# Gated-DeltaNet recurrence of a hybrid decoder block: the chunk inverse applied ahead of the loop, with a new stage order and other buffer counts

## The chip, the core and the metric

The kernel runs on one core of one Trainium2 chip. The metric is the device time of one execution in microseconds (us). Three runs of the kernel before gave a median of 2491.94 us (2491.32 to 2495.54).

## The reference

One decoder layer on 2048 tokens of width 1024. It normalises the input, projects it, and splits the columns between two groups of four heads of 128 columns. One group is a gated DeltaNet, the other a retention with fixed decay. Both outputs go through one output projection; a gated MLP with a causal convolution and a final norm follow. The change lies in the gated DeltaNet, whose core is this (per chunk; `m` is strictly lower triangular):

```python
m = jnp.where(strict, jnp.einsum('nbhik,nbhjk->nbhij', kb, kc) * decay, 0.0)
t_mat = lax.linalg.triangular_solve(eye + m, eye, left_side=True, lower=True, unit_diagonal=True)
u_base = jnp.einsum('nbhij,nbhjv->nbhiv', t_mat, vb)
w_mat = jnp.einsum('nbhij,nbhjk->nbhik', t_mat, kb * jnp.exp(gcum)[..., None])
...
def step(state, inp):
    u = u_b - jnp.einsum('bhck,bhkv->bhcv', w_c, state)
    o = jnp.einsum('bhck,bhkv->bhcv', qd_c, state) + jnp.einsum('bhij,bhjv->bhiv', qk_c, u)
    state = state * cd_c[..., None, None] + jnp.einsum('bhck,bhcv->bhkv', kd_c, u)
    return state, o
```

The state goes from chunk to chunk, so the steps of one head follow each other. Everything outside `step` can be done for all chunks at once.

## The kernel before

The tokens are worked in four blocks of 512, and each block in four chunks of 128 tokens. All products are in float32; the large ones are made of three products of values that are split in a high and a low part (`mm3` and `tokmajor`, three matmuls of 512 columns for each 128x128 tile of weights). After the four blocks come the MLP's up products (`mlp_up`, from about 1190 us on) and its down products (`mlp_down`).

A block consists of named stages, written out by hand in the string `ORDER` (L41): a digit for the block and a name. `pro` loads and norms x; `k0`, `q0`, `kq`, `v0` project for the retention heads and `h0` to `h3` are those heads (`ret_head`); `dec` and `d0` to `d3` make decays; `c0` to `c3` (`gdn_kq`, then `gdn_z`) and `e0` to `e3` (`gdn_v`) project, convolve and transpose keys, queries and values of the DeltaNet heads; `b0`, `b1` (`gdn_base`) and `l0`, `l1` (`gdn_lvls`) invert 1 + m for a pair of heads: 32x32 blocks by POOL, larger ones by small matmuls; `r00` to `r13` (`gdn_rec`) are the steps of the recurrence, first digit the pair, second the chunk; `p0`, `p1` and `G0`, `G1` are the gates and the gated outputs (`gated`), and `W1` to `W7` and `N` the output projection by seven products and the second norm. The string is the order in which the program is written. A scheduler then interleaves the stages on each engine, mostly so that pieces of the large products stand between the steps of the recurrence; each engine works through its own list in order. The numbers in `BUFS` and the constants `NW`, `NST` and `NACC` are caps on how many buffers of a kind are alive at once; tiles get their places from a common pool by lifetime.

A step of the recurrence (`gdn_rec`, L670 to L711) works on the two heads of a pair and has three hops from PE to DVE and back:

- `ks` (L684): keys times state and queries times state, four matmuls of 128x128 by 128. DVE subtracts the first, scaled, from the values `vp` (L687, one instruction for each head). ACT copies the second into the output `o` (L690).
- `wps` (L694): the inverse `TT` times those values, two matmuls. DVE scales the result by `brk` into `u` (L697).
- `sps` (L702): `kd` times `u`, then `A` times `u`, two matmuls each. DVE updates the states `Sst` (L704, one instruction for each head) and adds to `o` (L707). The next step's `ks` needs the states.

In the trace a float32 matmul is two instructions, so that a step shows 8, 4 and 8 of them on PE.

`ret_head` has a chain of its own: `rr` (L783) makes four products, L785 on DVE carries the retention state over the chunks, and each second `ro` matmul (L807) needs one of these states. `gated` multiplies the outputs into the gates (L421, DVE), transposes them (`mxt`, L423, PE), and ACT and DVE combine them into what the output projection `wo` reads through the split `wu` (L875, ACT). `dmat` loads a broadcast of the decays and finishes it on DVE (L492).

Weights come through `load_chunk` (L265). At the first use of a matrix the raw weights are loaded (L280) and split by ACT and DVE (L282, L283); from the use after `keep` becomes true the split parts are also written to DRAM, and later uses load them from there (L276). `NLATE` says how many matrices are not kept at their first use.

Of the kernel before, what the change touches and what calls it, by code (L numbers as in the profile page):

```python
# [10 lines left out]
AF = mybir.ActivationFunctionType  # L11
# [4 lines left out]
NW = 5  # L16
# [6 lines left out]
NST = 4  # L23
NUC = 7
NACC = 7
# [8 lines left out]
NLATE = 3  # L34
NXR = 7
FD = 4
BUFS = {"n1": 8, "ykq": 5, "kv": 4, "NT": 5, "AT": 8, "o": 2, "n2s": 11, "xk": 2, "og": 1, "co": 6, "Cw": 4,
        "wx": 1, "wsq": 3, "wvr": 3, "wvt": 9, "ca": 8, "mix": 10, "D": 8, "rk": 5, "rq": 4, "rv": 8,
        "Ar": 1, "Nb": 6, "rot": 1, "rrow": 7}

ORDER = ("0pro 0k0 0v0 0dec 0d0 0c0 0e0 0q0 0d1 0c1 0e1 0d2 0c2 0e2 0h0 0b0 0h1 0d3 0c3 0e3 0l0 0r00 0b1 "  # L41
# [8 lines left out]
P = 128  # L50
# [155 lines left out]
def mixers(ctx, tc, base, base_used, marks, drp, mm3, gamma, mhalf, n1w, n2w, gcw, gv127, epsr, gnw, n2d, hd,  # L206
# [116 lines left out]
    def small(nm, n=16, bufs=2):  # L323
        if nm not in ring:
            ring[nm] = [pc(bufs, n), 0, bufs]
        e = ring[nm]
        e[1] += 1
        return e[0][:, e[1] % e[2]]
# [13 lines left out]
    def A_items(b, st):  # L342
# [90 lines left out]
        def decays(_):  # L433
# [41 lines left out]
            neg = st["neg"] = small("neg", 16)  # L475
            DVE.tensor_scalar(neg, eg[:, :16], -1.0, None, op0=ALU.mult)
# [31 lines left out]
        def gdn_kq(h):  # L508
            def f(w):
# [19 lines left out]
                if ("brk", h // 2) not in st:  # L529
                    st["brk", h // 2] = small("brk", 8, 5)  # L530
                brk = hd_["brk"] = st["brk", h // 2][:, h % 2 * NT:(h % 2 + 1) * NT]
# [9 lines left out]
                kd = hd_["kd"] = half(hd_, "kv", "kv", 0)  # L541
                for c in range(NT):
                    ACT.activation(kd[:, c * P:(c + 1) * P], ps[:, c * P:(c + 1) * P], AF.Copy,
                                   scale=st["ed"][:, c * NH + h:c * NH + h + 1])
# [4 lines left out]
                for cc in range(2):  # L549
                    ps = mbank("kk")  # L550
                    for c1 in range(2):
                        c = cc * 2 + c1
                        PE.matmul(ps[:, c1 * 256:(c1 + 1) * 256].rearrange("p (a t) -> p a t", a=2),
                                  ykq[:, 0, c * P:(c + 1) * P], ykq[:, :, c * P:(c + 1) * P],
                                  start=True, stop=True)
                    for c1 in range(2):
                        c = cc * 2 + c1
                        DVE.scalar_tensor_tensor(Nt[:, c * P:(c + 1) * P], ps[:, c1 * 256:c1 * 256 + P],
                                                 nbrk[:, c:c + 1], Dm[:, c, :],
                                                 op0=ALU.mult, op1=ALU.mult)  # L560
                        DVE.tensor_tensor(At[:, c * P:(c + 1) * P], ps[:, c1 * 256 + P:c1 * 256 + 256],
                                          Dm[:, c, :], op=ALU.mult)
            return f

        def gdn_v(h):
            def f(w):
# [8 lines left out]
                vp = hd_["vp"] = half(hd_, "kv", "kv", 1)  # L575
# [93 lines left out]

        def gdn_rec(hs, c):  # L670
            def f(_):
# [8 lines left out]
                n = len(hs)  # L680
                ps = rbank("ks")
# [4 lines left out]
                for i, e in enumerate(H):  # L686
                    DVE.scalar_tensor_tensor(e["vp"][:, sl], ps[:, i * P:(i + 1) * P], st["neg"][:, jj[i]:jj[i] + 1],  # L687
                                             e["vp"][:, sl], op0=ALU.mult, op1=ALU.add)
# [3 lines left out]
                ps = rbank("wps")  # L692
                for i, e in enumerate(H):
                    PE.matmul(ps[:, i * P:(i + 1) * P], e["TT"][:, sl], e["vp"][:, sl], start=True, stop=True)  # L694
                h2 = lambda t: t.rearrange("p (i d) -> p i d", i=n)
                u = small("u", n * P, 2)
                DVE.tensor_tensor(h2(u), h2(ps[:, :n * P]),  # L697
                                  h2(st["brk", hs[0] // 2])[:, :, c:c + 1].to_broadcast([P, n, P]), op=ALU.mult)
# [122 lines left out]
        def g2(p):  # L821
            hs = (2 * p, 2 * p + 1)
            rec = [[(None, None, gdn_rec(hs, c))] for c in range(NT)]
            rec[-1].append((None, None, gdn_fin(hs)))
            return {f"l{p}": [(None, None, gdn_lvls(hs))]} | {f"r{p}{c}": r for c, r in enumerate(rec)}
# [456 lines left out]
```

## Time and profile before

| | |
|---|---|
| median of three runs | 2491.94 us |
| the profiled execution, by itself | 2488.28 us |
| its span, first to last instruction | 2486.5 us |
| mean granted TensorE clock | 0.992 |
| DVE busy | 1609.0 us (65%) |
| ACT busy | 997.9 us (40%) |
| POOL busy | 569.5 us (23%) |

The profiled execution took 1.8 us more than its span, and 3.66 us less than the median. In the profile PE is the matmul engine, PEld its weight loads, DVE VectorE, ACT ScalarE, POOL GpSimd. "Idle before" counts the time that an engine stood still ahead of an instruction, and names what ended it. A matmul's shown duration is longer than its turn in a stream, since the next one starts before it has ended.

### The profile page before, as it was taken

Reading aid. Unit: us, or ns where it says so; the run is one execution under the profiler, and the core shown is the slowest. Engines: PE = TensorE matmul, PEld = TensorE weight load, DVE = VectorE, ACT = ScalarE, POOL = GpSimd, SP = SyncE. Lnnn points to the kernel's source line nnn. Section 1 sums busy time; section 2 is a strip of 40 time slices with the busy share of each in tenths; the row PEclk is TensorE's granted clock in tenths of the full one; section 3 lists DMA queues with packets and bytes.
Section 4 is the critical chain, followed back from the end, with each engine's and each line's share of the span. In section 5 each row is a group of like instructions: output and inputs, shape, how many; then the busy total and the mean of one; then the engine's idle time right before and its main releaser. Section 6 shows DMA issues by size and latency. Waiting matters only on the chain. (4 is left out here: it accounts for less than half of the span.)

```text
span 2486.5 us, 35733 instructions
## 1 busy us (share of the span) xinstructions
PE 2413.2 (97%) x12476; PEld 2022.1 (81%) x12476; DVE 1609.0 (65%) x3132; ACT 997.9 (40%) x2149; POOL 569.5 (23%) x891
## 2 busy tenths in 40 slices
PE   8999899999999999998999999999999999999998
PEld 7877787888888978886788888888888888888877
DVE  5864776435653563537899889896556567554794
ACT  6644544434442552335454444442122234333331
POOL 1354146521047105230010000000000002430180
PEclk9999999999999999999999999999999999999999
DMA  8756499764864655645898888777667778764783
GB/s 327 265 195 220 167 338 321 265 220 151 306 214 161 207 211 202 225 146 200 333 342 334 297 300 298 287 280 250 226 241 254 273 268 268 233 207 140 251 275 115
DMA packets 285748, 610.17 MB, mean 245 GB/s; under 512 B 40896, under 2 KB 120960, under 8 KB 285568
## 3 DMA queue, kind: packets, MB, share of 16 engines
q1 hardware_dynamic: 269136, 593.85, 68.0%
q10 hardware_dynamic: 16432, 14.04, 1.8%
q8 instruction: 98, 1.61, 0.3%
q14 instruction: 82, 0.67, 0.1%
HBM read 411.09 MB, written 196.71 MB: 244 GB/s over the span
## 5 line engine op out<-in xcount | busy, mean ns | idle before, releaser
L115 PE MATMUL p<-x,wu 128*128 128x512 f32 x1176 | 458.9, 390 | 3.0 <-DVE x L932 2.9
L114 PE MATMUL p<-x,wu 128*128 128x512 f32 x1176 | 454.1, 391 | 4.2 <-ACT x L931 3.4
L116 PE MATMUL p<-x,wu 128*128 128x512 f32 x1176 | 451.1, 390 | 0.0
L386 PE MATMUL tok<-wc,n 128*128 128x512 f32 (+2 forms) x768 | 276.3, 363 | 11.5 <-ACT n L374 9.3
L387 PE MATMUL tok<-wc,n 128*128 128x512 f32 (+2 forms) x768 | 276.7, 361 | 0.0
L388 PE MATMUL tok<-wc,n 128*128 128x512 f32 (+2 forms) x768 | 274.4, 361 | 0.0
L114 PEld LDWEIGHTS p<-x,wu 128*128 128x128 f32 x1176 | 220.9, 188 | 53.0 <-ACT x L931 6.1
L115 PEld LDWEIGHTS p<-x,wu 128*128 128x128 f32 x1176 | 220.9, 188 | 50.9 <-DVE x L932 5.4
L116 PEld LDWEIGHTS p<-x,wu 128*128 128x128 f32 x1176 | 220.9, 188 | 45.4
L1052 DVE SCALAR_TENSOR_TENSOR acc<-uc,base,acc 128x1022 f32<-128x1022 f32 (+1 forms) x176 | 221.2, 1279 | 39.2 <-ACT acc L1049 37.7
L1010 DVE TENSOR_TENSOR uc<-p,uc 128x512 f32<-128x512 f32 x224 | 153.2, 686 | 134.0 <-PE p L116 131.7
L180 POOL TENSOR_TENSOR vt<-vr 128x512 f32<-128x512 f32 x44 | 69.1, 1573 | 625.2 <-DVE v L201 460.5
L114 PE MATMUL d<-v,uu 128*128 128x512 f32 x448 | 175.1, 391 | 0.0
L115 PE MATMUL d<-v,uu 128*128 128x512 f32 x448 | 175.0, 391 | 0.0
L116 PE MATMUL d<-v,uu 128*128 128x512 f32 x448 | 174.9, 390 | 0.0
L386 PEld LDWEIGHTS tok<-wc,n 128*128 128x128 f32 x768 | 146.3, 191 | 31.9 <-ACT n L374 9.3
L387 PEld LDWEIGHTS tok<-wc,n 128*128 128x128 f32 x768 | 146.6, 191 | 18.8
L388 PEld LDWEIGHTS tok<-wc,n 128*128 128x128 f32 x768 | 145.4, 191 | 19.3
L116 PE MATMUL chm<-n,wc 128*128 128x512 f32 x384 | 151.3, 394 | 0.0
L114 PE MATMUL chm<-n,wc 128*128 128x512 f32 x384 | 151.1, 394 | 0.0
L115 PE MATMUL chm<-n,wc 128*128 128x512 f32 x384 | 151.0, 393 | 0.0
L1057 POOL COPY base<-uc 128x2 f32<-128x2 f32 x44 | 31.9, 725 | 449.2 <-DVE uc L1010 449.2
(248 smaller groups left out, 4841.1 us busy)
## 6 DMA issues: line engine op xcount, KB each, us to landing
wu<-wu SPq DMA_DIRECT2D x308, 512.0 KB, 5.9
wc<-wd SPq DMA_DIRECT2D x168, 512.0 KB, 5.5
wv<-wo SPq DMA_DIRECT2D x84, 512.0 KB, 5.6
wd<-wc SPq DMA_DIRECT2D x60, 512.0 KB, 4.1
ur<-au SPq DMA_DIRECT2D x56, 512.0 KB, 5.8
wur<-in_w_u SPq DMA_DIRECT2D x44, 512.0 KB, 6.1
au<-st SPq DMA_DIRECT2D x88, 256.0 KB, 4.8
vr<-in_w_d SPq DMA_DIRECT2D x44, 512.0 KB, 5.9
```

Source lines behind the costliest of these rows:

```text
L114: PE.matmul(ps, ah, bh, start=(first and i == 0), stop=False, skip_group_check=chk)
L115: PE.matmul(ps, ah, bl, start=False, stop=False, skip_group_check=chk)
L116: PE.matmul(ps, al, bh, start=False, stop=(i == n - 1), skip_group_check=chk)
L180: POOL.tensor_tensor(tt[:, j], a, b_, op=ALU.subtract)
L386: PE.matmul(ps, ah, wh, start=(k == 0), stop=False)
L387: PE.matmul(ps, ah, wl, start=False, stop=False)
L388: PE.matmul(ps, al_, wh, start=False, stop=(k == KT - 1))
L1010: add = lambda o, ps, a: DVE.tensor_tensor(o, ps, a, op=ALU.add)
L1052: DVE.scalar_tensor_tensor(acc[:, t:], u[:, :T2 - t], w, acc[:, t:], op0=ALU.mult, op1=ALU.add)
L1057: POOL.tensor_copy(mhalo[:, ci], u[:, T2 - 2:])
```

## The change

The program's text changes in four places.

**The step has two hops.** A new stage `w0` or `w1` (`gdn_wy`) follows `l0` or `l1`. For each head and all four chunks it multiplies the inverse with decayed keys (`wy`) and with the values (`up`); ACT copies the first over the keys in `ykq`, DVE the second over `vp`. In `gdn_rec` the product `wps` and its scaling are gone, and one subtraction on both heads makes `u`.

**What the keys carry.** `gdn_kq` writes two scaled copies of the transposed keys instead of one: `kg` (by `eg`) for `wy` and `kd` (by `ed` times `brk`). `A` takes the factor `brk`, too. `neg` is no longer made.

**Order.** `ORDER` is another string. Among other moves `w0` and `w1` are put in, `0d2` stands ahead of `0q0`, and `3v0` is moved up ahead of `3k0`.

**Counts.** `NW` 5 to 6, `NST` 4 to 5, `NACC` 7 to 8, `kv` 4 to 5, `o` 2 to 4, `n2s` 11 to 12, `wsq` 3 to 5, `ca` 8 to 10, and `NLATE` 3 to 2: the third matrix (keys and queries of head 0) is kept at its first use.

```diff
-NLATE = 3
+NLATE = 2
...
-            neg = st["neg"] = small("neg", 16)
-            DVE.tensor_scalar(neg, eg[:, :16], -1.0, None, op0=ALU.mult)
...
-                kd = hd_["kd"] = half(hd_, "kv", "kv", 0)
+                eb = small("eb", 4, 5)
+                DVE.tensor_tensor(eb, st["ed"].rearrange("p (t h) -> p h t", h=NH)[:, h], brk, op=ALU.mult)
+                kd = hd_["kd"] = half(st, ("kd", h // 2), "kv", h % 2)
+                kg = hd_["kg"] = half(st, ("kg", h // 2), "kv", h % 2)
                 for c in range(NT):
-                    ACT.activation(kd[:, c * P:(c + 1) * P], ps[:, c * P:(c + 1) * P], AF.Copy,
-                                   scale=st["ed"][:, c * NH + h:c * NH + h + 1])
+                    j = c * NH + h
+                    ACT.activation(kg[:, c * P:(c + 1) * P], ps[:, c * P:(c + 1) * P], AF.Copy, scale=st["eg"][:, j:j + 1])
+                    ACT.activation(kd[:, c * P:(c + 1) * P], ps[:, c * P:(c + 1) * P], AF.Copy, scale=eb[:, c:c + 1])
...
-                        DVE.tensor_tensor(At[:, c * P:(c + 1) * P], ps[:, c1 * 256 + P:c1 * 256 + 256],
-                                          Dm[:, c, :], op=ALU.mult)
+                        DVE.scalar_tensor_tensor(At[:, c * P:(c + 1) * P], ps[:, c1 * 256 + P:c1 * 256 + 256],
+                                                 brk[:, c:c + 1], Dm[:, c, :], op0=ALU.mult, op1=ALU.mult)
...
+        def gdn_wy(hs):
+            def f(_):
+                for h in hs:
+                    e = st["hd", h]
+                    ps, ps1 = mbank("up"), mbank("wy")
+                    for c in range(NT):
+                        sl = slice(c * P, (c + 1) * P)
+                        PE.matmul(ps1[:, sl], e["kg"][:, sl], e["TT"][:, sl], start=True, stop=True)
+                        PE.matmul(ps[:, sl], e["TT"][:, sl], e["vp"][:, sl], start=True, stop=True)
+                    ACT.activation(e["ykq"][:, 0], ps1, AF.Copy)
+                    DVE.tensor_copy(e["vp"], ps)
+            return f
...
-                for i, e in enumerate(H):
-                    DVE.scalar_tensor_tensor(e["vp"][:, sl], ps[:, i * P:(i + 1) * P], st["neg"][:, jj[i]:jj[i] + 1],
-                                             e["vp"][:, sl], op0=ALU.mult, op1=ALU.add)
+                u = small("u", n * P, 2)
+                DVE.tensor_tensor(h2(u), st["vp", hs[0] // 2][:, :, sl], h2(ps[:, :n * P]), op=ALU.subtract)
...
-                ps = rbank("wps")
-                for i, e in enumerate(H):
-                    PE.matmul(ps[:, i * P:(i + 1) * P], e["TT"][:, sl], e["vp"][:, sl], start=True, stop=True)
-                h2 = lambda t: t.rearrange("p (i d) -> p i d", i=n)
-                u = small("u", n * P, 2)
-                DVE.tensor_tensor(h2(u), h2(ps[:, :n * P]),
-                                  h2(st["brk", hs[0] // 2])[:, :, c:c + 1].to_broadcast([P, n, P]), op=ALU.mult)
```

What the new order makes of the lists of the engines is shown at three places.

The first is PE at the end of the recurrence of block 2, second pair (steps `r12` and `r13`). In the kernel before these rows stand there, from the last matmul of a projection (`chm`) to the retention product `rr`:

```order
L116 MATMUL chm<-n_8630,wc 128x512
L694 MATMUL wps<-kv,AT 128x128 x2
L702 MATMUL sps<-pers_1359,kv 128x128 x2
L702 MATMUL sps<-pers_1359,AT 128x128 x2
L684 MATMUL ks<-pers_125,ykq 128x128 x4
L694 MATMUL wps<-kv,AT 128x128 x2
L702 MATMUL sps<-pers_1359,kv 128x128 x2
L702 MATMUL sps<-pers_1359,AT 128x128 x2
L783 MATMUL rr<-rv,rk 128x128 x4
```

In the changed kernel the last `sps` of the same pair stands between matmuls of a projection (`tok`), with `rr` and `rkk` of the retention heads behind it:

```order
L387 MATMUL tok<-wc,n_8693 128x264
L388 MATMUL tok<-wc,n_8693 128x264
L709 MATMUL sps<-pers_1390,kv 128x128 x2
L709 MATMUL sps<-pers_1390,AT 128x128 x2
L386 MATMUL tok<-wc,n_8698 128x264
L790 MATMUL rr<-rv,rk 128x128 x4
L806 MATMUL rkk<-ykq 128x128 x4
L387 MATMUL tok<-wc,n_8698 128x264
```

The groups of the two steps, which followed each other directly, now have projection matmuls between them; the same holds at the end of block 1.

The second is PE at the end of block 3, second pair, where no projection is left (`rtr` and `rkk` belong to a retention head). Before:

```order
L702 MATMUL sps<-pers_1359,AT 128x128 x2
L684 MATMUL ks<-pers_125,ykq 128x128 x4
L799 MATMUL rkk<-ykq 128x128 x4
L694 MATMUL wps<-kv,AT 128x128 x2
L702 MATMUL sps<-pers_1359,kv 128x128 x2
L702 MATMUL sps<-pers_1359,AT 128x128 x2
L684 MATMUL ks<-pers_125,ykq 128x128 x4
L694 MATMUL wps<-kv,AT 128x128 x2
L702 MATMUL sps<-pers_1359,kv 128x128 x2
L702 MATMUL sps<-pers_1359,AT 128x128 x2
L783 MATMUL rr<-rv,rk 128x128 x4
```

Now:

```order
L699 MATMUL ks<-pers_125,ykq 128x128 x4
L806 MATMUL rkk<-ykq 128x128 x4
L709 MATMUL sps<-pers_1390,kv 128x128 x2
L709 MATMUL sps<-pers_1390,AT 128x128 x2
L699 MATMUL ks<-pers_125,ykq 128x128 x4
L709 MATMUL sps<-pers_1390,kv 128x128 x2
L709 MATMUL sps<-pers_1390,AT 128x128 x2
L790 MATMUL rr<-rv,rk 128x128 x4
```

The `wps` rows are gone and the rest stands as before, without other work between.

The third is DVE at the end of block 0. L785 (L792 after the change) carries a retention state, L492 (L490) works on the decays of block 1 that a DMA brings, L421 multiplies outputs into gates. Before:

```order
L785 SCALAR_TENSOR_TENSOR pers_605<-pers_125,rr 128x128
L492 SCALAR_TENSOR_TENSOR D<-D,pers_230,base 128x128 x8
L719 SCALAR_TENSOR_TENSOR pers_605<-pers_605 128x8
L492 SCALAR_TENSOR_TENSOR D<-D,pers_230,base 128x128 x2
L785 SCALAR_TENSOR_TENSOR pers_605<-pers_605,rr 128x128
L492 SCALAR_TENSOR_TENSOR D<-D,pers_230,base 128x128 x6
L785 SCALAR_TENSOR_TENSOR pers_605<-pers_605,rr 128x128
L421 SCALAR_TENSOR_TENSOR mix<-o,pers_605,mix 128x128 x8
L785 SCALAR_TENSOR_TENSOR pers_125<-pers_605,rr 128x128
```

Now:

```order
L792 SCALAR_TENSOR_TENSOR pers_612<-pers_125,rr 128x128
L468 COPY pers_230<-pers_230 128x16
L470 TENSOR_TENSOR pers_230<-pers_230 128x16
L792 SCALAR_TENSOR_TENSOR pers_612<-pers_612,rr 128x128 x2
L421 SCALAR_TENSOR_TENSOR mix<-o,pers_612,mix 128x128 x4
L792 SCALAR_TENSOR_TENSOR pers_125<-pers_612,rr 128x128
L478 COPY pers_230<-gct 16x128
L421 SCALAR_TENSOR_TENSOR mix<-o,pers_612,mix 128x128 x8
```

The four links of the retention state now stand ahead of all work on the decays (L490), whose first row comes seven rows further down.

More of the change, by code (lines that the diff above doesn't have):

```diff
@@ L14 @@
 DRAM = bass.MemoryType.DRAM
-NW = 5
+NW = 6
 LA = 1
@@ L22 @@
 NWUR = 2
-NST = 4
+NST = 5
 NUC = 7
-NACC = 7
+NACC = 8
 NWU = 9
@@ L33 @@
 NRAW = 3
-NLATE = 3
+NLATE = 2
 NXR = 7
 FD = 4
-BUFS = {"n1": 8, "ykq": 5, "kv": 4, "NT": 5, "AT": 8, "o": 2, "n2s": 11, "xk": 2, "og": 1, "co": 6, "Cw": 4,
-        "wx": 1, "wsq": 3, "wvr": 3, "wvt": 9, "ca": 8, "mix": 10, "D": 8, "rk": 5, "rq": 4, "rv": 8,
+BUFS = {"n1": 8, "ykq": 5, "kv": 5, "NT": 5, "AT": 8, "o": 4, "n2s": 12, "xk": 2, "og": 1, "co": 6, "Cw": 4,
+        "wx": 1, "wsq": 5, "wvr": 3, "wvt": 9, "ca": 10, "mix": 10, "D": 8, "rk": 5, "rq": 4, "rv": 8,
         "Ar": 1, "Nb": 6, "rot": 1, "rrow": 7}
-ORDER = ("0pro 0k0 0v0 0dec 0d0 0c0 0e0 0q0 0d1 0c1 0e1 0d2 0c2 0e2 0h0 0b0 0h1 0d3 0c3 0e3 0l0 0r00 0b1 "
[8 rows of a table removed]
+ORDER = ("0pro 0k0 0v0 0dec 0d0 0c0 0e0 0d2 0q0 0d1 0c1 0e1 0c2 0e2 0d3 0h0 0b0 0h1 0c3 0l0 0w0 0b1 0r00 "
[8 rows of a table added]
 P = 128
@@ L528, in f @@
                 DVE.tensor_scalar(ss, ss, EPS, None, op0=ALU.add)
-                if ("brk", h // 2) not in st:
-                    st["brk", h // 2] = small("brk", 8, 5)
-                brk = hd_["brk"] = st["brk", h // 2][:, h % 2 * NT:(h % 2 + 1) * NT]
+                brk = hd_["brk"] = small("brk", 4, 8)
                 nbrk = hd_["nbrk"] = small("nbrk", 4, 8)
@@ L574, in f @@
                     PE.transpose(ps[:, c * P:(c + 1) * P], acc[:, c * P:(c + 1) * P], ident)
-                vp = hd_["vp"] = half(hd_, "kv", "kv", 1)
+                vp = hd_["vp"] = half(st, ("vp", h // 2), "kv", h % 2)
                 for c in range(NT):
@@ L680, in f @@
                 n = len(hs)
+                h2 = lambda t: t.rearrange("p (i d) -> p i d", i=n)
                 ps = rbank("ks")
@@ L824, in g2 @@
             rec[-1].append((None, None, gdn_fin(hs)))
-            return {f"l{p}": [(None, None, gdn_lvls(hs))]} | {f"r{p}{c}": r for c, r in enumerate(rec)}
+            return {f"l{p}": [(None, None, gdn_lvls(hs))], f"w{p}": [(None, None, gdn_wy(hs))]} | {f"r{p}{c}": r for c, r in enumerate(rec)}
         def rh(h):
```

16 rows, old and new, of the table ORDER are left out of this document.

## The prediction

> **What bounds the kernel now.** I read the page's first lines, then the busy time by stretches, then PE's idle time by group, then single places in order of time.
>
> ```profile
> span 2486.5 us, 35733 instructions
> PE 2413.2 (97%) x12476; PEld 2022.1 (81%) x12476; DVE 1609.0 (65%) x3132; ACT 997.9 (40%) x2149; POOL 569.5 (23%) x891
> ```
>
> PE is the bound: it is busy for 97% of the span and stands still for 73.3 us. The stretches (columns: PE, weight loads, DVE, ACT, POOL, then granted clock, DMA share, GB/s) say where.
>
> ```profile
> 0.00:1190.00 1190.00, 1130.83 (x6830) 963.13 (x6831) 673.79 (x1861) 532.65 (x1459) 401.93 (x750) 0.99 0.65 230
> 1190.00:2430.00 1240.00, 1233.46 (x5432) 1018.79 (x5431) 912.01 (x1233) 456.14 (x668) 163.18 (x133) 1.00 0.77 267
> 50.00:100.00 50.00, 50.00 (x280) 43.61 (x278) 39.13 (x94) 31.80 (x81) 6.41 (x10) 1.00 0.84 286
> 200.00:250.00 50.00, 45.45 (x349) 39.12 (x349) 27.14 (x70) 24.06 (x66) 18.25 (x46) 0.93 0.52 180
> 250.00:300.00 50.00, 38.60 (x256) 34.53 (x255) 33.34 (x127) 29.34 (x86) 8.47 (x12) 0.90 0.43 158
> 850.00:900.00 50.00, 44.30 (x269) 38.00 (x268) 33.31 (x110) 27.69 (x77) 5.95 (x8) 0.97 0.40 137
> 1100.00:1150.00 50.00, 44.08 (x399) 38.91 (x398) 25.18 (x80) 24.22 (x81) 2.66 (x2) 1.00 0.18 64
> 1150.00:1200.00 50.00, 40.55 (x171) 29.82 (x171) 44.83 (x90) 28.28 (x62) 2.64 (x2) 0.97 0.89 335
> ```
>
> Up to 1190 us, where the mixers end, PE idles 59.2 us; behind that 6.5 us in 1240. The idle time sits at the ends of the blocks (200 to 300, 850 to 900, 1100 to 1200), where the projections have run out and the recurrence is left with nothing to fill its hops. There the clock falls below 1 too. So the MLP stays as it is, and the mixers decide. Next, PE's idle time by group and by what ended it (us in total, times, longest):
>
> ```profile
> L684 PE MATMUL ks<-pers,ykq 128*128 128x128 f32 x256 | 35.8, 282 | 7.4 <-DVE pers L704 3.7 <-DVE AT L561 1.3 <-DVE o L707 1.1
> L694 PE MATMUL wps<-kv,AT 128*128 128x128 f32 x128 | 21.9, 293 | 4.5 <-DVE kv L687 3.1 <-ACT o L690 1.4
> L702 PE MATMUL sps<-pers,kv 128*128 128x128 f32 x128 | 20.6, 283 | 6.3 <-DVE pers L697 5.3 <-ACT o L690 0.6 <-DVE pers L476 0.4
> ...
> PE tok L386 <- ACT n L374: 9.3, 1, 9.3
> PE wo L114 <- ACT wu L875: 6.3, 4, 1.9
> PE ro L807 <- DVE pers L785: 5.8, 5, 2.9
> PE mxt L423 <- DVE mix L421: 3.6, 4, 1.6
> PE ro L806 <- DVE Ar L800: 1.5, 1, 1.5
> ```
>
> The recurrence has 7.4 + 4.5 + 6.3 = 18.2 us; 9.3 us is the start of the program.
>
> **The change part by part.** First, what is added on PE. Per pair of heads and chunk `wps` had two matmuls and `wy` with `up` have four; with 4 blocks, 2 pairs and 4 chunks that is 64 more, or 128 instructions, as the trace shows two for each. Their price comes from one unfilled step in block 3:
>
> ```profile
> 1116.67 1.16 PE L684 MATMUL ks<-pers,ykq 128*128 128x128 f32 x8
> 1117.87 0.61 DVE L687 SCALAR_TENSOR_TENSOR kv<-ks,pers,kv 128x128 f32<-128x128 f32 x2 [0.34 <-PE ks L684]
> 1118.36 0.68 PE L694 MATMUL wps<-kv,AT 128*128 128x128 f32 x4 [0.54 <-DVE kv L687]
> 1119.08 0.42 DVE L697 TENSOR_TENSOR pers<-wps,pers 128x256 f32<-128x256 f32 x1 [0.61 <-PE wps L694]
> 1119.56 0.71 PE L702 MATMUL sps<-pers,kv 128*128 128x128 f32 x4 [0.52 <-DVE pers L697]
> 1121.16 1.20 PE L684 MATMUL ks<-pers,ykq 128*128 128x128 f32 x8 [0.44 <-DVE pers L704]
> 1125.09 1.06 PE L783 MATMUL rr<-rv,rk 128*128 128x128 f32 x8
> ```
>
> The eight of `rr` run in 1.06 us; one alone lasts 0.28 (the `ks` row), so the next starts (1.06 - 0.28) / 7 = 0.112 us later. 128 x 0.112 = **14.3 us more PE work**. Nothing hides it, since PE is the bound.
>
> The same rows give what a hop costs without filler. From `ks` to `ks` pass 1121.16 - 1116.67 = 4.49 us, in which 8 + 4 + 8 = 20 instructions take 2.24. So 2.25 us are lost while the brackets show 0.54 + 0.52 + 0.44 = 1.50: a stop costs 1.5 times its idle time, since the last matmul drains. The recurrence's 18.2 us stand for 27 us lost, about 36 unfilled hops of 0.75.
>
> How many are left? At the ends of blocks 1 and 2 the new list of PE has projection work between all groups; its steps need fillers for two hops, not three, and the projections last longer. At the end of block 3 the list still has bare hops (`ks` to `sps`, `sps` to `ks`, `ks` to `sps`), at the end of block 0 three or four, and `wy` stands close behind the last level of the inverse twice. I count 10 or 11, 8 us. **Gain 19 us**; from 6.8 (only the 4.5 of `wps` go, times 1.5) to 27.
>
> Second, other waits at these ends, which the new lists fill or reorder:
>
> ```profile
> 282.23 0.49 PE L807 MATMUL ro<-pers,ykq 128*128 128x128 f32 x2 [1.46 <-DVE pers L785]
> 285.82 0.79 PE L807 MATMUL ro<-pers,ykq 128*128 128x128 f32 x2 [2.89 <-DVE pers L785]
> 283.83 1.14 DVE L492 SCALAR_TENSOR_TENSOR D<-D,pers,base 128x128 f32<-128x128 f32 x4 [0.61 <-DMA D<-gdr]
> 888.51 1.06 PE L423 MATMUL mxt<-base,mix 128*128 128x128 f32 x8 [0.70 <-DVE mix L421]
> 891.51 0.50 PE L114 MATMUL wo<-wv,wu 128*128 128x512 f32 x1 [1.94 <-ACT wu L875]
> ```
>
> In block 0 `ro` waits since L785 is queued behind decays that wait for a DMA; in the new DVE list it stands ahead of them: 4.4 us back. In block 2 `chm` matmuls now stand between `mxt` and `wo`: 2.6 us back. With the 1.5 of L800, which now has `tok` matmuls to cover it, I take **9 us**; from 0 to 12.
>
> Third, the clock. The rows 0.93, 0.90, 0.97 and 0.97 above lack (0.07 + 0.10 + 0.03 + 0.03) x 50 = 11.5 us of PE cycles, part of them while PE stood still anyway. If half of the stops go I take back **6 us**; from 0 to 11.5. The Trainium skill, "TensorE: Matmul & The Clock Gate" (What's actually happening), gives an idle window of about 3.4 us as what halves the clock. The trace disagrees in so far as no wait of PE but the first is longer than 2.89 us, and the clock fell in four stretches; by the page's threshold those stops would not be the cause and this term would be 0.
>
> Fourth, the costs beside PE. ACT gets 64 copies for `kg` and 16 of 128x512 for `wy`; DVE loses 64 + 32 instructions and gets 32 + 16.
>
> ```profile
> L690 ACT ACTIVATE o<-ks,pers 128x128 f32<-128x128 f32 x64 | 20.1, 367 | 42.5 <-DVE kv L687 38.6 <-issue 2.5 <-DVE pers L719 0.7
> L809 ACT ACTIVATE o<-ro 128x512 f32<-128x512 f32 x16 | 9.5, 592 | 10.9 <-PE ro L807 10.9
> L687 DVE SCALAR_TENSOR_TENSOR kv<-ks,pers,kv 128x128 f32<-128x128 f32 x64 | 19.5, 345 | 30.7 <-PE ks L684 30.5
> L697 DVE TENSOR_TENSOR pers<-wps,pers 128x256 f32<-128x256 f32 x32 | 13.5, 422 | 34.7 <-PE wps L694 34.6
> L505 DVE TENSOR_TENSOR ca<-chm,rrow 128x512 f32<-128x512 f32 x48 | 33.0, 688 | 34.9 <-PE chm L116 32.1 <-ACT pers L526 1.6 <-ACT ykq L519 0.8
> L558 DVE SCALAR_TENSOR_TENSOR NT<-kk,pers,D 128x128 f32<-128x128 f32 x64 | 22.0, 343 | 1.1
> L561 DVE TENSOR_TENSOR AT<-kk,D 128x128 f32<-128x128 f32 x64 | 17.9, 280 | 0.0
> ```
>
> ACT: 64 x 0.367 + 16 x 0.592 = +33 us, beside 533 of 1190 busy. DVE: -64 x 0.345 - 32 x 0.422, then +32 x 0.422, 16 x 0.688 and 64 x (0.343 - 0.280) for `A`: -7 us. Both lie under PE's projections. But `kd` now needs `brk`, thus the squares of keys and queries, and holds the bank with the transposed keys that long; behind it wait the next transposes and ACT's queue. The new lists differ in thousands of rows and will have stops of their own. By the rows from nothing to as many as `wo`, `mxt` and L800 have now (6.3 + 3.6 + 1.5, with drain 17); I take **7 us**, near the `wo` row.
>
> Fifth, `NLATE`: 4 x 512 KB are written in block 0 instead of block 1, where the DMA engines were busy for 0.84 and moved 286 GB/s (50 to 100 us); 2.1 MB take 7.3 us of them. The sixth buffer of `NW` covers part; in block 1 two raw loads, four splits on ACT and DVE go, which PE did not wait for. **2 us**, from 0 to 7. The other counts I cost at nothing, since PE waits on no DMA in these rows and a free buffer can only start a load earlier; if the lists needed them, that is in the waits above.
>
> The sum: 14.3 - 19 - 9 - 6 + 7 + 2 = -10.7 us on the execution's 2488.3 us (span 2486.5 and 1.8 around it): 2477.6. That execution lies 3.7 us under the median of 2491.9, so I forecast **2481 us**.
>
> **The rivals.** *The removed hop was hidden, and the work is not.* Where fillers stand, a hop costs nothing, and 2 of 3 hops remain where they don't. If only the waits ahead of `wps` go (6.8 us) and the rest stays as it is, the time is 2488.3 + 14.3 - 6.8 = 2495.8, or 2499 beside the median: slower. It decides from the point where less than 14.3 us of stops are won. For it: the row of `wps` has only 4.5 us. Against it: the lists, where the groups at the ends of blocks 1 and 2 no longer touch.
>
> *The stops move.* ACT's 33 us and the longer hold on the transposes cost 1 us for each of 16 heads-in-blocks: 7 becomes 16, and 2490 follows, no change. Against it: ACT has over half its time free.
>
> *The clock stays.* The stops that remain still trip it, and the 6 us are not won: 2487, at the border of no change. For it: blocks 0 and 3 keep bare hops. Against it: a block end without stops, such as the new one of block 2, leaves nothing to trip it. By the threshold of the Trainium skill's page above, the short stops that go were not what tripped it, and the time would be this one.
>
> *All of it comes.* The fillers close all hops but 4 us' worth, the clock is back: 14.3 - 23 - 12 - 9 + 4 = -25.7, so 2466. For it: the stops are few and in places where the list has changed.
>
> **How the numbers follow.** A measurement of this kernel tells about 0.2% (5 us) from no change. Chances: forecast 0.48, all of it 0.14, the clock stays 0.14 (half faster, half the same), the stops move 0.09, the hidden hop 0.15. Faster 0.48 + 0.14 + 0.07 = 0.69, same 0.16, slower 0.15. The range leaves out half of the outermost cases on both sides: 2467 to 2498.
>
> **What would show it.** PE's busy work: 128 more instructions in `wy` and `up`, the sum of instructions 12604. The idle rows of `ks` and `sps` should fall from 13.7 to about 6 us and no `wps` row be left; 850 to 900 should be busy at clock 1.00; L807's wait should shrink to under 2 us; PE's idle up to the MLP to about 35 us. I am wrong if that idle time stays near 59 us, if a row of `kqtr`, `chm` or `tok` waiting on ACT appears with several us, or if the first 100 us lengthen.

## The result and the profile after

The changed kernel takes 2496.74 us (median of 20 runs, 2490.44 to 2504.17) against 2491.03 us for the kernel before (20 runs on the same chip): a ratio of **1.0025, with a 95% interval of 1.0016 to 1.0034**, slower by 0.25%. The forecast was 2481 us, faster. The time lies inside the range, but on the other side of no change.

The head of the page of the changed kernel:

```profile
span 2493.8 us, 36020 instructions
PE 2427.1 (97%) x12604; PEld 2035.8 (82%) x12604; DVE 1606.6 (64%) x3092; ACT 1026.8 (41%) x2227; POOL 586.9 (24%) x891
```

PE is busy for 13.9 us more than before (2427.1 against 2413.2), and the span is 7.3 us longer: 6.6 us of idle time were won, where the sum had counted on 25 us of stops and clock. The busy time by stretches of the changed kernel, for the stretches that the prediction quoted and those that changed most (columns: length, then PE, weight loads, DVE, ACT, POOL, then granted clock, DMA share, GB/s):

```profile
0.00:1190.00 1190.00, 1140.29 (x6955) 976.71 (x6956) 668.66 (x1816) 559.93 (x1535) 409.79 (x750) 0.99 0.65 229
1190.00:2430.00 1240.00, 1230.68 (x5418) 1013.47 (x5416) 909.26 (x1230) 454.14 (x665) 172.11 (x132) 1.00 0.77 267
250.00:300.00 50.00, 44.61 (x322) 39.84 (x322) 40.46 (x143) 34.39 (x101) 9.29 (x13) 1.00 0.42 156
350.00:400.00 50.00, 47.71 (x213) 38.94 (x212) 36.97 (x81) 25.51 (x75) 13.97 (x14) 0.97 0.84 301
600.00:650.00 50.00, 47.75 (x229) 39.97 (x228) 31.89 (x90) 24.97 (x63) 2.65 (x2) 0.93 0.67 235
850.00:900.00 50.00, 50.00 (x354) 46.30 (x353) 16.80 (x61) 22.67 (x77) 5.00 (x5) 1.00 0.43 143
1000.00:1050.00 50.00, 47.83 (x237) 39.47 (x236) 21.73 (x68) 24.05 (x81) 18.35 (x40) 1.00 0.63 223
1100.00:1150.00 50.00, 48.60 (x418) 43.76 (x417) 21.34 (x61) 25.20 (x78) 2.77 (x3) 1.00 0.29 102
```

Three of these stretches of the kernel before, which the prediction had not looked at because nothing was lost in them or they seemed untouched:

```profile
350.00:400.00 50.00, 50.00 (x232) 41.48 (x232) 42.10 (x86) 26.78 (x75) 15.48 (x15) 1.00 0.92 329
600.00:650.00 50.00, 48.04 (x244) 40.05 (x245) 36.36 (x108) 26.48 (x71) 4.14 (x4) 1.00 0.76 265
1000.00:1050.00 50.00, 50.00 (x251) 42.30 (x250) 21.79 (x77) 19.11 (x62) 11.69 (x20) 1.00 0.67 228
```

The block ends that the prediction aimed at are better: 38.60 of 50 us busy became 44.61 (250 to 300), 44.30 became 50.00 (850 to 900), 44.08 became 48.60 (1100 to 1150). But 350 to 400 and 1000 to 1050 had no gap before and have one now, and the clock falls at 600. The idle time up to 1190 us went from 59.2 to 49.7 us, not to the 35 us that the prediction named; in the MLP behind it, it rose from 6.5 to 9.3.

To compare stretches in which both work and clock differ, I use one measure below. Each shape of matmul instruction has an undisturbed distance to the start of the next one, read from filled stretches (0.2265 us with 512 columns, 0.1195 with 264, 0.111 with 128, less for the small ones). **PE work** is the sum of these distances over all PE instructions of a trace, and **lost time** is what the starts lie further apart than that: waits, the drain around them, and half clock together. Before: 2361.3 us of work and 108.2 lost. After: 2375.5 and 100.8. So the work grew by 14.2 us and the loss shrank by 7.4; with 0.6 us of later start that is the 7.3 us of span. Lost us by stretch, where it moved by 1 us or more:

| stretch from | 10 | 100 | 150 | 200 | 250 | 350 | 400 | 450 | 500 | 550 | 600 | 850 | 1000 | 1100 | 1150 | 1200 | 1250 |
|---|---|---|---|---|---|---|---|---|---|---|---|---|---|---|---|---|---|
| before | 2.4 | 2.0 | 4.0 | 9.2 | 18.3 | 0.2 | 5.7 | 2.5 | 1.3 | 4.0 | 3.3 | 9.9 | 0.2 | 10.7 | 15.5 | 1.4 | 2.1 |
| after | 1.4 | 0.3 | 7.6 | 8.1 | 8.9 | 4.6 | 8.0 | 4.7 | 2.7 | 1.3 | 5.9 | 0.4 | 3.4 | 3.3 | 17.3 | 3.4 | 3.3 |

(The last stretch runs to 2400 us.) All falls together are 34 us, all rises 26. The prediction had 19 + 9 + 6 = 34 us of falls and 7 + 2 = 9 of rises.

The recurrence itself, in the groups of PE of the changed kernel (busy us, mean ns | idle us ahead, and what ended it):

```profile
L699 PE MATMUL ks<-pers,ykq 128*128 128x128 f32 x256 | 35.7, 276 | 1.2 <-DVE pers L711 1.1
L709 PE MATMUL sps<-pers,kv 128*128 128x128 f32 x128 | 20.7, 285 | 2.7 <-ACT o L704 1.4 <-DVE pers L702 1.3
```

18.2 us of idle time in three groups became 3.9 in two. What PE waits for now (total us, times, longest):

```profile
PE mxt L423 <- DVE mix L421: 5.5, 3, 2.7
PE p L115 <- DVE x L939: 4.5, 5, 1.9
PE wo L115 <- DVE wv L201: 4.4, 1, 4.4
PE ro L813 <- DVE Ar L807: 3.7, 2, 3.1
PE wo L114 <- ACT wu L882: 3.5, 2, 2.2
PE chm L114 <- DVE ca L503: 2.1, 1, 2.1
PE vtr L574 <- DVE AT L561: 1.5, 1, 1.5
```

None of these is the recurrence. Several are single waits of 1.5 to 4.4 us, and but for `vtr`, which waits for `A`, they are in operations that the change does not touch. The longest of them, at 447 us, shows how such a wait is read. First PE, then DVE ahead of it, in the changed kernel:

```profile
446.77 0.80 PE L115 MATMUL wo<-wv,wu 128*128 128x512 f32 x1 [4.42 <-DVE wv L201]
```

```profile
441.26 0.21 DVE L338 SCALAR_TENSOR_TENSOR ca<-pers,base,ca 128x1 f32<-128x1 f32 x1
443.53 0.71 DVE L621 STREAM_TRANSPOSE NT<-AT 128x512 f32<-128x512 f32 x1 [2.06 <-DMA AT<-z]
444.16 0.81 DVE L334 SCALAR_TENSOR_TENSOR ca<-ca,base 128x510 f32<-128x510 f32 x1
444.90 1.21 DVE L338 SCALAR_TENSOR_TENSOR ca<-pers,base,ca 128x2 f32<-128x2 f32 x1
446.04 0.68 DVE L201 TENSOR_TENSOR wv<-wvt,wv 128x512 fp32r<-128x512 f32 x1
```

PE needs L201, the low half of a split weight. It stands on DVE behind a transpose that waits 2.06 us for the DMA of the inverse's base, and behind two steps of a convolution. DVE is busy for 64% of the span, and still PE waits for it: an engine that takes its instructions in order holds whatever stands behind a wait. How much of the 4.42 us that hold is worth, e14 tells below.

### The profile page after: what moved, and what is told of

Same layout as the page of the kernel before. It is cut to its first block, busy times and chain, and to the rows that moved or that the text cites. A ratio compares the mean times of both kernels' runs of the same rounds, so it can differ in the third digit from the quotient of the medians.

```text
span 2493.8 us, 36020 instructions
## 1 busy us (share of the span) xinstructions
PE 2427.1 (97%) x12604; PEld 2035.8 (82%) x12604; DVE 1606.6 (64%) x3092; ACT 1026.8 (41%) x2227; POOL 586.9 (24%) x891
## 5 line engine op out<-in xcount | busy, mean ns | idle before, releaser
L115 PE MATMUL p<-x,wu 128*128 128x512 f32 x1176 | 458.6, 390 | 4.5 <-DVE x L939 4.5
L115 PEld LDWEIGHTS p<-x,wu 128*128 128x128 f32 x1176 | 220.9, 188 | 52.7 <-DVE x L939 7.3
L115 PE MATMUL d<-v,uu 128*128 128x512 f32 x448 | 175.2, 391 | 0.0
L115 PE MATMUL chm<-n,wc 128*128 128x512 f32 x384 | 151.9, 396 | 0.0
L1064 POOL COPY base<-uc 128x2 f32<-128x2 f32 x44 | 41.6, 946 | 444.6 <-DVE uc L1017 444.6
```

What stands on the lines that cost most here:

```text
L115: PE.matmul(ps, ah, bl, start=False, stop=False, skip_group_check=chk)
L1064: POOL.tensor_copy(mhalo[:, ci], u[:, T2 - 2:])
```

## The experiments

All ratios are to the kernel before, run beside it, with the 95% interval; PE work and lost time (us) are those of one profiled execution each. Thirteen kernels ran.

In most of them the scheduler laid the engines' lists anew, because an instruction or a step of `ORDER` had changed. Of the 12348 PE instructions that e9 shares with the kernel before, some 2600 stand in another place in its trace; in e6 it is some 1900 of 12476, in e7, against the changed kernel, some 3600 of 12348. So these runs don't change one thing alone. e11 and e14 come close to that (50 to 75 of 12604 against the changed kernel).

| kernel | hops | ratio | PE work | lost |
|---|---|---|---|---|
| before | 3 | 1 | 2361.3 | 108.2 |
| after | 2 | 1.0025 | 2375.5 | 100.8 |
| e1: new code, old order and counts | 2 | 1.0149 | 2375.5 | 128.2 |
| e3: new code and counts, old order | 2 | 1.0321 | 2375.5 | 176.0 |
| e4: new code and order, old counts | 2 | 1.0044 | 2375.5 | 110.3 |
| e2: old code, new order and counts | 3 | 1.0048 | 2361.3 | 122.7 |
| e5: after with `NLATE` 3 | 2 | 1.0072 | 2375.5 | 117.8 |
| e6: before with unread products | 3 | 1.0164 | 2389.7 | 123.9 |
| e7: after without `wy` and `up` | 2 | 0.9900 | 2347.1 | 98.8 |
| e9: before without `wps` | 2 | 0.9906 | 2347.1 | 103.5 |
| e10 to e13: after, one thing moved | 2 | 1.0019 to 1.0092 | 2375.5 | 98.2 to 114.0 |
| e14: after, one DMA not awaited | 2 | 1.0011 | 2375.5 | 98.2 |

**The two parts alone: e9, e7, e6.** The first takes the third hop out of the program and adds nothing to it:

```
-                    DVE.scalar_tensor_tensor(e["vp"][:, sl], ps[:, i * P:(i + 1) * P], ...)
+                    DVE.scalar_tensor_tensor(u[:, i * P:(i + 1) * P], ps[:, i * P:(i + 1) * P], ...)
...
-                ps = rbank("wps")
-                for i, e in enumerate(H):
-                    PE.matmul(ps[:, i * P:(i + 1) * P], e["TT"][:, sl], e["vp"][:, sl], start=True, stop=True)
-                DVE.tensor_tensor(h2(u), h2(ps[:, :n * P]), ..., op=ALU.mult)
```

> The kernel before, old order and counts, with the inverse's product and the scaling by brk left out of the step, so that it has two hops and 128 PE instructions less: part of the computation is left out. The work alone is 14.3 us. If removing the hop wins the stops that the prediction counts (18 to 20 us, and the clock), 33 to 40 us less than before (2452 to 2458); if the hop was hidden, 14 to 20 us less (2472 to 2477).

Measured: 2467.83 us, ratio 0.9906 (0.9893 to 0.9919), 22.6 us under the kernel before beside it. Of these 14.2 us are the 128 PE instructions that are gone, so **the hop as a stop, together with the lists that come of leaving it out, was worth some 8 us**: 6 to 12 by the interval, 5 by lost time in the one profiled execution. That lies between the two expectations. Its waits are nearly gone, but others came or grew: `wo` at 281 us (2.7), `p` at 1146 us (3.7) and, in the middle of block 1, `tok` at 478 us (3.5). PE's waits in e9, then the one recurrence group of note:

```profile
PE wo L114 <- ACT wu L870: 8.6, 6, 2.7
PE p L114 <- ACT x L926: 5.9, 3, 3.7
PE tok L386 <- DVE rq L734: 3.5, 1, 3.5
PE rkk L794 <- ACT ykq L789: 3.3, 2, 2.2
```

```profile
L684 PE MATMUL ks<-pers,ykq 128*128 128x128 f32 x256 | 35.3, 281 | 3.1 <-DVE pers L699 1.8 <-DVE AT L561 1.2
```

The row of `ks` fell from 7.4 to 3.1 us, `sps` from 6.3 to 0.4, and the 4.5 of `wps` are gone: 15 us of idle time. Lost time ahead of these groups fell by 19 us, from 29.6 to 10.2. The total lost only fell from 108.2 to 103.5. The stretches from 200 to 310 us and from 840 to 940 lost 14 us less; those from 400 to 500 and from 560 to 640 and the MLP lost some 10 more.

e7 takes the products out of the changed kernel, so that `ykq` and `vp` are read unmultiplied:

```
-            return {f"l{p}": [...], f"w{p}": [(None, None, gdn_wy(hs))]} | ...
+            return {f"l{p}": [...], f"w{p}": []} | ...
```

> The changed kernel without the products ahead of the recurrence and their copies, so that keys and values enter the steps without the inverse: part of the computation is left out. 256 instructions less on PE: 28.7 us less than the changed kernel (2468) if all of their work is on the path; 2475 or more if they fill stops or if the lists differ by themselves.

Measured: 2464.00 us, ratio 0.9900 (0.9886 to 0.9914). That is 0.0125 or 31 us under the changed kernel, for 28.4 us of work, so the products cost their work in full. The lost time stays in sum (98.8 against 100.8), but not in its places: the waits at 367 and 447 us are gone, and others at 410, 414, 470 and 1007 us have come. A two-hop kernel without the products loses as much in stops.

e6 adds the same number of products, whose result nothing reads, to the kernel before:

```
+            PE.matmul(ps1[:, sl], e["kd"][:, sl], e["TT"][:, sl], start=True, stop=True)
+            PE.matmul(ps[:, sl], e["TT"][:, sl], e["vp"][:, sl], start=True, stop=True)
```

> The kernel before, with 128 matmuls of 128x128 by 128 for each of the two products added behind l0 and l1, whose results are not read: 256 instructions of each kind, 512 of PE in all where the change adds a net 128. By the step of 0.112 us the whole is 28.7 us for 256 instructions; both theories expect 26 to 30 us more than before if nothing hides it, and 20 or less if the products fill bare hops.

The expectation counts the instructions twice over: the page shows 12732 on PE, 256 more than before. Measured: 2531.16 us, 1.0164 (1.0151 to 1.0178), or 41 us, more than either theory. The profiled execution is 44 us over that of the kernel before, of which 28.4 are work and 16 more lost time. The work is hidden nowhere, and an order that was not made for it adds stops.

As a sum, -22.6 (e9) + 28.4 (the products' work) is +5.8 us, and the change measures +5.7. That they agree is luck as far as these runs tell: e1 below, the same two parts in the old order, measures +37 us, and e6 alone +41.

**Code, order and counts: e1, e3, e4, e2.** e1 has the new functions with the old `ORDER` and counts (the new steps `w0`, `w1` directly behind `l0`, `l1`), e3 the new counts with that order, e4 the new order with the old counts; e2 leaves the functions and takes the new order (without `w`) and counts.

```
e1: ORDER = <before, "l0 w0", "l1 w1">; NW, NST, NACC, NLATE, BUFS of before but "kv": 5
e3: ORDER = <before, "l0 w0", "l1 w1">
e4: NW, NST, NACC, NLATE, BUFS of before but "kv": 5
e2: the kernel before with ORDER of after without w0, w1; NW, NST, NACC, NLATE, BUFS of after
```

> Two hops with the old order (w0 and w1 put in right behind l0 and l1) and the old counts (kv 5, which the pairwise tiles need). Theory A, the new lists brought the stops that ate the gain: 14.3 us of work, some 18 us of recurrence stops won, no other change, so 0 to 8 us faster than before (ratio 0.997 to 1.000). Theory B, the removed hop was hidden and the work is not: 6 to 14 us slower (1.0025 to 1.006).

> Two hops with the old order (w0, w1 behind l0, l1) and the new counts. Theory A1, the order is what the two-hop step needs: as slow as two hops with old order and old counts, 30 us or more over before (1.012 or more). Theory A2, the counts are what it needs: within 10 us of before (0.998 to 1.004).

> Two hops with the new order and the old counts (kv 5). Theory A1, the order decides: within 6 us of the changed kernel (1.000 to 1.005 of before). Theory A2, the counts decide: 20 us or more over before (1.008 or more).

> Three hops as before, with the new order (without w0 and w1) and the new counts. Theory A: slower than before by the stops that the new lists bring, 8 to 15 us (1.003 to 1.006). Theory B: within 4 us of before (0.9985 to 1.0015), since order and counts do little.

Measured: e1 2527.40 us (1.0135 to 1.0163), e3 2570.43 us (1.0308 to 1.0335), e4 2502.58 us (1.0033 to 1.0056), e2 2502.65 us (1.0034 to 1.0061). e1 is slower than both of its theories; the others are where their first theory put them. The order, not the code, sets whether the stops are won: with the old order the two-hop step loses 20 to 68 us more than three hops did. Behind the start of the program, these rows hold the longest wait of e1 and that of e3:

```profile
PE sps L701 <- ACT o L696: 10.0, 3, 7.6
```

```profile
PE nps L909 <- ACT n2s L910: 40.9, 3, 36.5
```

In both PE waits for ACT, and ACT for something else; the rows of ACT, e1 and then e3:

```profile
218.77 0.62 ACT L696 ACTIVATE o<-ks,pers 128x128 f32<-128x128 f32 x2 [14.31 <-POOL pers L600]
```

```profile
540.32 1.26 ACT L910 ACTIVATE n2s<-nps,base 128x512 f32<-128x512 f32 x2 [34.69 <-POOL pers L600]
```

L600 is a line of POOL's loop of 31 steps for the base of an inverse: the trace names it for both, while neither of the ACT rows reads its result. Its last row in e1 is the last that reads `Nb`, the copy of the matrix that is inverted:

```profile
218.53 0.21 POOL L600 TENSOR_TENSOR pers<-Nb,pers 128x8 f32<-128x8 f32 x1
```

It ends at 218.74 us, and ACT starts at 218.77; in e3 the last one ends at 540.29 and ACT starts at 540.32. `o`, `n2s` and `Nb` are tiles of one size from one pool. So the rows fit a wait for the place that `Nb` had held, and not for the inverse. The trace doesn't say which place a tile got, so this stays a reading.

With the new order the counts are worth 0.0019 (e4 against after). The new order doesn't help the old code either: e2 loses 14.5 us more than before. With the order of the other code, three hops cost 12 us more and two hops 31 (e1, which has the old counts, too) or 74 (e3). That each order is fitted to its code is my reading of these four runs; how the orders were found is not on record.

**`NLATE`: e5.** The changed kernel with `NLATE = 3`.

> The changed kernel with NLATE back at 3, so that the third matrix is not written in block 0. If the early writes cost what the prediction took, 2 us less than the changed kernel (2495); if the writes are behind the stops between 150 and 250 us, 5 to 8 us less (2489); if only the lists are laid anew, anything within 10 us.

Measured: 2509.23 us, 1.0072 (1.006 to 1.0083), 12 us over the changed kernel and outside all three expectations. Lost time rose by 17 us, nearly all of it between 100 and 550 us, a time in which many lists were laid anew. The term of the prediction (2 us that `NLATE` 2 costs) had the wrong sign in this order; as a price of the DMA traffic it could not be told from the lists that it lays anew.

**One instruction moved: e10.** The split behind which PE waits at 447 us goes to POOL:

```
-    v = split_v(nc, mk("v", F32R), src)
+    v = split_v(nc, mk("v", F32R), src, kept is not None and i == 4 and k == 1)
...
-    nc.vector.tensor_tensor(v[:, 1], src, ...)
+    (nc.gpsimd if pool else nc.vector).tensor_tensor(v[:, 1], src, ...)
```

> The changed kernel with one instruction moved: the low half of one wv split (block 0, product 4, k 1) is made by POOL instead of by DVE. In the changed kernel PE waits 4.42 us for it at 447 us (wo L115 behind DVE L201), because it stands on DVE behind a transpose that waits for the DMA of the inverse's base. Theory (the new stops come from in-order queues in which something that waits for a DMA stands ahead of what PE needs): that wait shrinks to under 1 us, lost time from 400 to 500 us falls from 12.7 to about 8 us, and up to 2430 PE instructions the rest of the stretches up to 1190 us stays as it is within 3 us; in total 0 to 5 us less than the changed kernel. Rival (DVE's queue is not the cause, PE would wait for something else at the same place): the wait is there under another name, and 400 to 500 us loses 12 us or more as before.

Measured: 2506.54 us, 1.0072 (1.0058 to 1.0086). PE in e10:

```profile
446.12 0.50 PE L115 MATMUL wo<-wv,wu 128*128 128x512 f32 x1 [1.60 <-POOL wv L201]
451.12 1.11 PE L521 MATMUL kqtr<-base,ykq 128*128 128x128 f32 x4 [3.82 <-ACT ykq L517]
```

The wait shrank from 4.42 to 1.60 us (expected: under 1), and 5 us later PE waits 3.82 us for the convolution that stands behind the same transposes. 400 to 500 us loses 14.9 us instead of 12.7: the rival was right on the stretch. The other 10 us of the total came behind 1250 us (13.7 lost instead of 3.3), in the MLP, whose entry was laid anew in the lists though nothing in it was meant to change.

**The hold taken away: e14.** The two transposes of block 1, pair 0 read a matrix that is there already, which leaves the right inverse of that pair out:

```
-                    DVE.transpose(T, TT)
+                    DVE.transpose(T, hd_["N"] if (b, p) == (1, 0) else TT)
```

> The changed kernel in which the two transposes of the inverse's base (L621) of block 1, pair 0 read the matrix N, ready long before, and not the base that comes by DMA: this leaves the right inverse of that pair out, with as many instructions as before. In the lists these two transposes stand 75 and 150 rows of DVE earlier and the rest around 450 us is as it was. Theory (one hold: DVE waits 2.06 us for that DMA ahead of the convolution and the split that PE needs): the 4.42 us wait of wo L115 at 447 us shrinks to 2 us or less, no wait of kqtr takes its place, 400 to 500 us loses 9 us or less instead of 12.7, and the kernel is 3 to 5 us faster than the changed one. Rival (the stretch is short of ready work in any case, or the split waits for ACT and POOL): wo L115 or a neighbour waits 4 us or more as before, 400 to 500 us loses 12 us or more.

Measured: 2492.64 us, 1.0011 (1.0002 to 1.002). PE in e14, and its stretches:

```profile
447.27 0.50 PE L115 MATMUL wo<-wv,wu 128*128 128x512 f32 x1 [2.73 <-DVE wv L201]
...
449.76 1.11 PE L521 MATMUL kqtr<-base,ykq 128*128 128x128 f32 x4 [1.29 <-ACT ykq L517]
```

```profile
400.00:450.00 50.00, 44.29 (x220) 36.73 (x219) 26.51 (x56) 20.74 (x58) 43.85 (x74) 0.99 0.69 230
450.00:500.00 50.00, 50.00 (x324) 41.13 (x324) 21.27 (x73) 15.22 (x41) 21.98 (x38) 0.95 0.73 274
```

Between the theories: lost time in 400 to 500 us is 10.9 (expected 9 or less, rival 12 or more). The hold makes up 1.7 of the 4.42 us; the other 2.73 remain, for the split still stands behind the convolution, which began when `chm` was done. The wait at 457 us (`vtr`, 1.5) is gone. So the DMA hold is one cause, worth 1.7 us of this wait; that the stretch has too little ready work around it is the likely other, which no run tested by itself. The whole kernel is no faster than e11 below, which keeps the hold (1.0019, the intervals overlap).

**Other orders nearby: e11, e12, e13.** One step of the changed kernel's `ORDER` moved, the rest left:

```
e11: "1d2 1b0 1e3 0W4 1c2 1e2 1h0"  ->  "1d2 1e3 0W4 1c2 1e2 1h0 1b0"
e12: "1dec 0G1"  ->  "0G1 1dec"
e13: "0w0 0b1 0r00 0e3"  ->  "0w0 0r00 0e3 0b1"
```

> The changed kernel with one step of ORDER moved: 1b0 stands behind 1h0 instead of ahead of 1e3. The instruction lists differ from the changed kernel's in some twenty rows of DVE, ACT and POOL around 450 us and at the entry of the MLP. Theory (the time hangs on the places of single instructions): within 6 us of the changed kernel, with the difference in the stretches 400 to 500 and 1150 to 1250 us; one direction or the other. Rival (only the code's dependences count): within 2 us, and no stretch differs by more than 1 us.

> The changed kernel with two neighbours of ORDER swapped: 0G1 ahead of 1dec. All lists are laid anew from about 290 us to 500 us and at the entry of the MLP, with the same work. Theory (any new laying of these lists has stops of its own, some 20 us over a list that was searched for): the stops at 365 and 447 us go or change, others come, lost time stays between 95 and 115 us, time 2490 to 2508. Rival (the changed kernel's order is as good as before's, and the new stops belong to the two-hop code): the same stops at the same places, time within 3 us of the changed kernel.

> The changed kernel with one step of ORDER moved: 0b1 stands behind 0e3, not behind 0w0. All lists are laid anew from about 160 us on, with the same work. Theory (any new laying has stops of its own): the stops at 163, 284, 365 and 447 us go or change and others come; lost time 95 to 120 us, time 2490 to 2513. Rival (the stops belong to the two-hop code): the same stops by name, time within 3 us of the changed kernel.

Measured: 1.0019 (1.001 to 1.0028), 1.0043 (1.0031 to 1.0056) and 1.0092 (1.0078 to 1.0106), with 98.2, 106.0 and 114.0 us lost. e11, in which some 75 PE rows stand elsewhere, is the changed kernel again. In e12 the stop at 365 us went (350 to 400: 0.2 us lost instead of 4.6) and 5.1 us came between 300 and 350; in e13 350 to 450 loses 2.2 instead of 12.6, and 500 to 550 12.2 instead of 2.7, where this wait of e13 has come:

```profile
PE nps L917 <- ACT n2s L918: 8.1, 3, 4.2
```

Not all stops move: `ro` still waits for `Ar` at 166 us in e12. The same work loses 98 to 114 us in these three orders and the changed kernel's, mostly in places that move, so most of the new stops belong to how the lists fall and not to the two-hop code as such. No order tried makes the two-hop code faster than the kernel before; whether one exists stays open.

## Why the prediction was wrong, point by point

*PE work, 14.3 us more:* right (14.2 by the distances, 13.9 in busy time), and hidden nowhere (e6, e7).

*The recurrence, 19 us back:* right. Idle time of its groups fell from 18.2 to 3.9 us, which at 1.5 is 21 us; lost time ahead of them fell by 22, from 29.6 to 7.6. No `wps` row is left, and `ks` with `sps` went from 13.7 to 3.9 where about 6 was expected.

*Other waits at the block ends, 9 us:* half right. The wait of `ro` for the retention state is gone, so are those of `mxt` and `wo` at 888 to 892 us, and 850 to 900 is full at clock 1.00. But `ro` for `Ar`, which was to be covered, grew from 1.5 to 3.7 us, and `mxt` now waits 1.2 and 2.7 us at the end of block 0. These rows with `wo` for `wu` went from 17.2 us of idle time to 12.7, so 4.5 came back. That all falls by stretch come to 34 us, as the first three terms did, is partly luck: a stretch holds falls and rises together.

*The clock, 6 us:* wrong, 0. PE ran at half clock for 27.3 us up to the MLP, before and after. It left 267, 285 and 892 us and came at 166, 368 and 614; the 6.8 us at 216 became 3.4 at 231, and the 3.4 us at 428 became 6.8 at 446. The prediction was right that the short stops trip the clock (in the kernel before, PE idled 1.5 to 2.7 us in the 3.4 us ahead of each fall; see the last section), but the new stops trip it as well. What was won in the old places was paid in the new ones.

*The costs beside PE, 7 us, "near the `wo` row":* **this is the step that failed.** Rises of 26 us stand against 9 with the `NLATE` term. I had bounded the new stops by the `wo`, `mxt` and L800 rows of the old lists (17 us with drain), as if a list that changes in thousands of rows could at worst lose as much in new waits as three groups of the old order still had. e2 shows what a foreign order costs that code (14.5 us more lost), and the other lists that hold all of the work lose 98 to 176 us; both kernels of this study stand near the low end. The change took out of the recurrence what it said; e9 shows the same in the old order: 19 us of lost time leave the recurrence and 5 us are gained in all. Two reasons are not told apart there, other chains that end next when PE has nothing else ready, and lists laid anew. That such chains trail because the projections, which fill PE, are a fixed amount is my reading; no run varied them.

*`NLATE`, 2 us:* wrong in sign in this order (e5), without a price of its own that could be told apart.

*The rivals.* None came as it was put. "The hidden hop" gave the nearest time (2499) with another mechanism: the hop was not hidden, its stops did go, and others came. "The stops move" had the mechanism but put it on ACT's copies and a longer hold on the transposes; the waits are on DVE at least as much (`mxt`, `wo` L115, `ro`, `chm`), and none of `kqtr` on ACT is on the list. "The clock stays" was right on the clock, but its 2487 holds the new stops at 7 us, as the forecast did.

## What to carry to other kernels

When a change swaps stops for work on the bound engine, count the work in full and of the stops only what is left when the next chain of the same stretch is late: the one run that takes the hop out and adds nothing (here e9, some 8 us against the 27 estimated from the idle rows) gives a first size before the rest is built, with the lists that it lays anew in it. In a program whose order is written out by hand for its code, a new order brings new stops of its own, and their size is to be taken from what neighbouring orders lose, not from the waits of the old one. A lone wait of several us is read by walking up the in-order queue of the engine that is waited for; moving the one instruction that PE named here (e10) handed most of the wait to the next behind the same hold.

## What the runs showed of the hardware

The clock was granted in whole windows. In the changed kernel it was halved from 446.40 to 453.20 us, from inside the wait of 4.42 us that ended at 446.77; in e1 for 23.90 us from 215.70, inside that wait of 7.64 us that ended at 219.45. First the changed kernel, then e1:

```profile
446.40:453.20 6.80, 6.43 (x17) 4.81 (x18) 6.28 (x12) 3.31 (x11) 2.95 (x3) 0.50 0.84 280
```

```profile
215.70:239.60 23.90, 14.14 (x53) 12.18 (x54) 6.11 (x15) 6.74 (x25) 2.94 (x12) 0.50 0.06 14
```

Every stretch of half clock in the mixers of these traces is 3.4 us or a multiple (6.8, 10.2, 13.7, 17.1, 23.9, 47.8), and within it the clock is 0.50. The Trainium skill, "TensorE: Matmul & The Clock Gate" (What's actually happening), describes just that: two states, half and full, and a free-running window of 3413 ns. The traces agree with both. They don't agree with the idle window of about 3.4 us that the page gives for the fall to half: in e14 the longest wait near 447 us is 2.73 us, and the clock was halved for 6.8 us from 448.6 all the same.

What halves it can be worked out from the traces. In each, the changes of the clock lie on one grid of 3.413 us steps. Without the first 14 and the last 10 us of PE's work, the fifteen traces hold 10591 such windows at full clock. All 95 in which PE stood idle for 1.86 us or more were followed by half clock, none of the 10355 with less than 1.2 us were, and 29 of the 141 between. The idle time is that of the profile, in which the ends of matmuls are modelled.

That the same stop halves the clock in one run and not in another shows in the changed kernel and e11, whose lists are alike there. The changed kernel, then e11, then e11's stretch:

```profile
613.67 0.80 PE L114 MATMUL wo<-wv,wu 128*128 128x512 f32 x1 [2.25 <-ACT wu L882]
```

```profile
612.90 0.50 PE L114 MATMUL wo<-wv,wu 128*128 128x512 f32 x1 [2.25 <-ACT wu L882]
```

```profile
600.00:650.00 50.00, 47.75 (x245) 40.21 (x245) 33.90 (x94) 27.77 (x77) 2.65 (x2) 1.00 0.71 252
```

The wait is 2.25 us in both, and the stretch has a clock of 0.93 in the one and 1.00 in the other: 3 us of lost time hang on how the stop lies against the window. In the changed kernel 2.19 us of it lie in the window that ends at 613.6 us; in e11 a border of the grid at 611.8 us cuts it into 1.15 and 1.10.

POOL made the low half of a 128x512 split in 1.29 us (e10), DVE in 0.68.
